# Mean squares of an RMS norm: squares taken by ScalarE from the PSUM bank, two halves of the features added by Pool, high and low parts in the rows of one product

## The chip, the cores and the metric

The kernel runs on one core of a Trainium2 chip. The metric is the device time of one execution in microseconds; the time before is the median of three runs. The engines are TensorE (PE for its products, PEld for its weight loads), VectorE (DVE), ScalarE (ACT), GpSimd (Pool or POOL) and the queue SP, which only issues DMAs. Each engine takes its instructions in the order in which the program lists them.

## The reference, cut to what matters

One layer of a streaming encoder with three groups of heads works on 1024 prompt tokens and 8 x 16 sample tokens. Group B is a differential attention with four heads, each 128 values wide. Its output goes through an RMS norm over the 128 features of a head, and that norm's mean of squares is what the change computes in another way:

```python
def diff_post(o, g, lambda_init):
    of = o.astype(jnp.float32)
    of = of * lax.rsqrt(jnp.mean(of * of, -1, keepdims=True) + RMS_EPS) * g.astype(jnp.float32) * (1.0 - lambda_init)
    return of.astype(o.dtype)
...
        o_b = diff_post(diff_attention_prompt(bq, bk, bv, lam), diff_subln_g[layer], lambda_init)
...
        s_b = diff_post(diff_core(tq, tk_all, tv_all, lam, None), diff_subln_g[layer], lambda_init)
```

The rest of the layer is one input projection (3584 columns), group A (banded attention, two units of two heads), group M (attention into 256 memory tokens, two units), a gate, an output projection and a layer norm.

## The kernel before, in words

Everything is float32. A product on TensorE takes float32r operands, and to keep float32 accuracy each operand is split into a high part (a float32r copy) and a low part (the value minus its copy). So each projection is three products into one bank (L155, L156, L157: high x high, low x high, high x low).

The work goes through eight units, in the order M0, B0, B1, B2, B3, A0, A1, M1. In each unit the attention over the prompt is the main stream, and projections (of gates, values, and the next unit's queries) are merged into it as fill; the 128 sample tokens of a unit are worked through in stages while the next unit's keys are projected. The program is written in that order, and a scheduler then reorders the instructions of each engine by its own estimate of times; so an edit of a few lines moves rows on every engine. What it makes of this change is shown below from the order of instructions.

For a B unit, `attention_b` goes over four pairs of 128 query columns. Scores are two products (L467, L468) into a bank of the pool `ps`; DVE takes the maximum (L604), ScalarE the exponential (L609). The weights are transposed by TensorE (L480) into a bank of the pool `pt` (two banks), split by ScalarE and DVE (L483/L487, L484/L488), and multiplied with the values into the one bank `po` (L643). When a pair is complete, `post_b` is called on the bank: it holds 128 features (partitions) by 256 tokens. `mean_square` queues the sum over the features as a product with a column of 1/128 (`mean`), so that the result is one row of 256 numbers; this small product is put between the products of a projection, or is forced out at the end of a pair. The row's bank is again `po`; DVE copies it to SBUF (L512) and SP stores it.

For the 128 sample tokens of a B unit, the last stage transposes the outputs (L908) into a `pt` bank, calls `post_b` on it with n = 128, and the row of mean squares goes into another `pt` bank. So the two banks of `pt` are shared by the sample's stages, by the transposes of the weights (L480) and by those of the values (L431): the next transposes wait until `post_b` has read the one bank and L512 the other.

In `post_b` before, ScalarE copies the bank to `od` (L495), Pool squares `od` (L499), ScalarE makes the float32r copy (L500), Pool the low part (L501), and TensorE takes two products, of the high and of the low part (L510). There are 4 pairs and 1 sample block in each of 4 units: 20 calls, 16 with n = 256 and 4 with n = 128.

At the end, the output projection (L1082) runs for nine tiles of 128 tokens; the first two are merged into the last unit. For a tile, `load` fetches its gates and mixed outputs back from DRAM, and `gated` scales them (L1049 on DVE).

Of the kernel before, what the change touches and what calls it, by code (L numbers as in the profile page):

```python
# [7 lines left out]
F32 = mybir.dt.float32  # L8
F32R = mybir.dt.float32r
AF = mybir.ActivationFunctionType  # L10
ALU = mybir.AluOpType
# [4 lines left out]
P = 128  # L16
# [59 lines left out]
def hybrid_step(tc, d, o):  # L76
    nc = tc.nc
    ctx = ExitStack()

    def pool(name, bufs=1, **kw):  # L80
        return Pool(ctx.enter_context(tc.tile_pool(name=name, bufs=bufs, **kw)))

    def f(ap):
        return ap.bitcast(F32)
# [22 lines left out]
    mean = const.tile([P, 1], F32R, tag="mean")  # L107
# [192 lines left out]
    tmp = pool("tmp", 2)  # L300
# [9 lines left out]
    for i in range(2):  # L310
        nc.vector.tensor_tensor(
            out=dl[:, i * 128 : i * 128 + 64], in0=dl[:, i * 128 : i * 128 + 64],
            in1=dl[:, i * 128 + 64 : i * 128 + 128], op=ALU.mult)
# [146 lines left out]
    def keep(u, a, b, od):  # L460
        nc.sync.dma_start(
            oscr[a // P : b // P, :, u.slot].rearrange("t p c -> p t c"), od.rearrange("p (t c) -> p t c", c=P))
# [29 lines left out]
    def post_b(u, po, c0, n):  # L492

        od = tmp.tile([P, n], F32, tag=f"od{n}", bufs=n // P)
        nc.scalar.copy(od, po)  # L495
        hi = tmp.tile([P, 256], F32R, tag="sqh", bufs=1)
        lo = tmp.tile([P, 256], F32R, tag="sql", bufs=1)
        sq = tmp.tile([P, 4, P], F32, tag="rs", bufs=2).rearrange("p a b -> p (a b)")[:, :n]
        nc.gpsimd.tensor_tensor(out=sq, in0=od, in1=od, op=ALU.mult)  # L499
        nc.scalar.copy(hi[:, :n], sq)  # L500
        nc.gpsimd.tensor_tensor(out=lo[:, :n], in0=sq, in1=f(hi)[:, :n], op=ALU.subtract)  # L501
        keep(u, c0, c0 + n, od)
        return hi, lo, sq[0:1]

    def mean_square(u, sq, ms, c0, n):


        def go():
            for x in range(2):
                nc.tensor.matmul(ms[:, :n], lhsT=mean, rhs=sq[x][:, :n], start=(x == 0), stop=(x == 1))  # L510
            row = sq[2]
            nc.vector.tensor_copy(row, ms[:, :n])  # L512
            nc.sync.dma_start(mscr[u.idx, c0 // P : (c0 + n) // P].rearrange("(o t) c -> o (t c)", o=1), row)

        tiny.append(go)
# [70 lines left out]
    def attention_b(u, need):  # L586
# [32 lines left out]
        def pair(j):  # L619
# [25 lines left out]
            def end():  # L645
                sq = post_b(u, st["po"], j * 256, 256)
                ms = ps_o.tile([1, 256], F32, tag="po")
                mean_square(u, sq, ms, j * 256, 256)
# [141 lines left out]
    def sample(u, kc_src, vc_src, nmask):  # L790
# [114 lines left out]
        def back():  # L905

            pt = ps_t.tile([P, P], F32, tag="pt")
            nc.tensor.transpose(pt, st["ot"], ident)  # L908
            if kind == "B":
                st["sq"] = post_b(u, pt, NPR, P)  # L910
            else:
                od = u.out[:, NPR:NTOK] if u.slot == 7 else tmp.tile([P, P], F32, tag="od128", bufs=1)
                nc.vector.tensor_copy(od, pt)
                if u.slot < 7:
                    keep(u, NPR, NTOK, od)
# [422 lines left out]
```

## Time and profile before

| | before |
|---|---|
| median of three runs | 669.27 us (666.96 to 670.08) |
| the profiled execution | 668.79 us, span 667.0 us from its first to its last instruction |
| PE busy | 653.6 us, 98% of the span |
| PEld busy | 611.0 us, 92% |
| DVE, ACT, POOL busy | 468.5 us (70%), 354.3 us (53%), 225.9 us (34%) |
| DMA | 78.91 MB, 118 GB/s on average |

Busy time is the time in which an engine had an instruction under way. The rows of products overlap each other, so PE's busy share doesn't say by itself that products follow each other at full rate; the distance from one product's start to the next one's does. The span is shorter than the execution's time by what lies around it, 1.8 us here.

### The profile page before, as it was taken

How to read it: one execution, taken by the hardware profiler on the slowest of the kernel's cores; microseconds unless marked ns; L12 is line 12 of the kernel's file. 1: busy time of each engine (PE TensorE's matmuls, PEld its weight loads, DVE VectorE, ACT ScalarE, POOL GpSimd, SP SyncE). 2: the span in 40 equal slices, each digit the busy share in tenths (PEclk: the TensorE clock that was granted, in tenths of full speed). 3: DMA queues.
4: the chain of work that ended last, by engine and by line, in shares of the span. 5: the costliest groups of instructions: out<-in, count | busy, mean ns of one | idle time of the engine just before them, and what ended most of it. 6: DMA issues, size and time to landing. Idle time of an engine off the chain costs nothing.

```text
span 667.0 us, 12222 instructions
## 1 busy us (share of the span) xinstructions
PE 653.6 (98%) x4306; PEld 611.0 (92%) x4306; DVE 468.5 (70%) x1173; ACT 354.3 (53%) x922; POOL 225.9 (34%) x278
## 2 busy tenths in 40 slices
PE   8999999999999999999999999999999999999995
PEld 7999999999899999998999999999999997887885
DVE  4769867787587757887477516674466688998755
ACT  5857854656455654566456635664466586211000
POOL 8253222642254223632324234332233142253101
PEclk9999999999999999999999999999999999999998
DMA  8951442121312232132312123132323747875311
GB/s 274 306 182 53 147 143 64 40 86 64 94 59 84 69 100 76 38 120 93 104 61 72 52 95 77 40 115 80 119 68 104 250 140 237 323 267 176 129 63 64
DMA packets 55837, 78.91 MB, mean 118 GB/s; under 512 B 9384, under 2 KB 33504, under 8 KB 55776
## 3 DMA queue, kind: packets, MB, share of 16 engines
q1 hardware_dynamic: 55488, 77.73, 35.3%
q8 instruction: 34, 0.56, 0.3%
q10 hardware_dynamic: 288, 0.39, 0.2%
q14 instruction: 27, 0.22, 0.1%
HBM read 57.69 MB, written 20.42 MB: 117 GB/s over the span
## 4 chain that ended last, share of the span: by engine, by line
PE 85%; DMA 6%; DVE 4%; issue 2%; ACT 1%; POOL 1%; SPq 0%; DVEq 0%; POOLq 0%; ACTq 0%
PE pp L155 15%; PE pp L157 15%; PE pp L156 15%; PE pp L1082 9%; PE ps L1082 6%; PE pt L480 5%; PE ps L467 4%; PE ps L468 4%; PE po L643 4%; PE po L682 3%; DMA rh<-in_wout 2%; PE pt L898 1%; DMA p<-mixed 1%; PE pt L431 1%; DMA mraw<-in_wmem 1%
## 5 line engine op out<-in xcount | busy, mean ns | idle before, releaser
L155 PE MATMUL pp<-xh,whi 128*128 128x384 f32 x594 | 203.7, 343 | 0.0
L156 PE MATMUL pp<-xl,whi 128*128 128x384 f32 x594 | 202.5, 341 | 0.0
L157 PE MATMUL pp<-xh,wlo 128*128 128x384 f32 x594 | 202.2, 340 | 0.0
L155 PEld LDWEIGHTS pp<-xh,whi 128*128 128x128 f32 x594 | 111.8, 188 | 2.7 <-DVE t L454 0.3
L156 PEld LDWEIGHTS pp<-xl,whi 128*128 128x128 f32 x594 | 111.8, 188 | 2.0 <-issue 0.2
L157 PEld LDWEIGHTS pp<-xh,wlo 128*128 128x128 f32 x594 | 111.8, 188 | 1.9 <-issue 0.3
L140 POOL TENSOR_TENSOR wlo<-wraw,whi 128x512 fp32r<-128x512 f32 x54 | 75.3, 1417 | 72.8 <-ACT whi L139 72.8
L609 ACT ACTIVATE p<-ps,nm 128x512 f32<-128x512 f32 (+3 forms) x96 | 55.2, 579 | 54.1 <-DVE nm L606 35.6
L467 PE MATMUL ps<-ka,qa 128*128 128x512 f32 (+4 forms) x176 | 58.6, 338 | 0.5 <-DVE nm L716 0.5
L468 PE MATMUL ps<-kl,qa 128*128 128x512 f32 (+4 forms) x176 | 57.4, 329 | 0.0
L480 PE MATMUL pt<-ident,p 128*128 128x128 f32 x332 | 54.9, 274 | 1.6 <-DVE ptl L484 0.8
L604 DVE TENSOR_REDUCE nm<-ps 128x1 f32<-128x512 f32 (+3 forms) x96 | 50.9, 549 | 4.0 <-PE ps L468 2.6
L724 POOL TENSOR_SCALAR p<-p,rs 128x640 f32<-128x640 f32 (+4 forms) x32 | 21.4, 671 | 68.7 <-DVE rs L723 52.7
L480 PEld LDWEIGHTS pt<-ident,p 128*128 128x128 f32 x332 | 39.9, 140 | 5.0 <-DVE ptl L484 2.1
L484 DVE TENSOR_TENSOR ptl<-pt,pth 128x512 fp32r<-128x512 f32 x56 | 38.3, 683 | 5.5 <-ACT pth L483 5.0
L483 ACT CAST pth<-pt 128x512 fp32r<-128x512 f32 x56 | 32.6, 586 | 17.3 <-PE pt L480 13.5
L1082 PE MATMUL pp<-xh,whi 128*128 128x512 f32 (+1 forms) x96 | 36.5, 380 | 0.0
L1082 PE MATMUL pp<-xl,whi 128*128 128x512 f32 (+1 forms) x96 | 36.2, 377 | 0.0
L1082 PE MATMUL pp<-xh,wlo 128*128 128x512 f32 (+1 forms) x96 | 35.8, 377 | 0.0
L139 ACT CAST whi<-wraw 128x512 fp32r<-128x512 f32 x54 | 30.9, 618 | 8.5 <-PE pp L156 4.5
L467 PEld LDWEIGHTS ps<-ka,qa 128*128 128x128 f32 x176 | 33.2, 189 | 1.8 <-DVE nm L716 0.7
L643 PE MATMUL po<-pth,va 128*128 128x256 f32 (+1 forms) x160 | 34.5, 284 | 0.0
(258 smaller groups left out, 1422.3 us busy)
## 6 DMA issues: line engine op xcount, KB each, us to landing
wraw<-in_win SPq DMA_DIRECT2D x54, 256.0 KB, 3.2
xr<-in_xT SPq DMA_DIRECT2D x12, 384.0 KB, 5.8
gates<-t SPq DMA_DIRECT2D x24, 192.0 KB, 2.2
qa<-in_xn SPq DMA_DIRECT2D x9, 512.0 KB
out_y<-qa SPq DMA_DIRECT2D x16, 256.0 KB, 2.2
mixed<-od SPq DMA_DIRECT2D x28, 128.0 KB, 2.3
p<-gates SPq DMA_DIRECT2D x7, 512.0 KB
p<-mixed SPq DMA_DIRECT2D x7, 448.0 KB
```

The source lines that it names most:

```text
L140: eng.tensor_tensor(out=lo[:, h], in0=raw, in1=f(hi[:, h]), op=ALU.subtract)
L155: nc.tensor.matmul(ps, lhsT=w[0][:, k], rhs=xh_[:, k], start=(k == 0), stop=False)
L156: nc.tensor.matmul(ps, lhsT=w[0][:, k], rhs=xl_[:, k], start=False, stop=False)
L157: nc.tensor.matmul(ps, lhsT=w[1][:, k], rhs=xh_[:, k], start=False, stop=(k == KT - 1))
L467: nc.tensor.matmul(ps, lhsT=u.qa[h][:, qs], rhs=u.ka[h][:, k0 : k0 + n], start=True, stop=False)
L468: nc.tensor.matmul(ps, lhsT=u.qa[h][:, qs], rhs=kl[h][:, k0 : k0 + n], start=False, stop=True)
L480: nc.tensor.transpose(pt[:, t, q * P : (q + 1) * P], p[q][:, cols[t][q] : cols[t][q] + P], ident)
L484: nc.vector.tensor_tensor(out=lo, in0=pt, in1=f(hi), op=ALU.subtract)
L604: nc.vector.tensor_reduce(out=nm[:, m, c : c + 1], in_=ps[c][:, : b - a], axis=AX.X, op=ALU.max, negate=True)
L609: nc.scalar.activation(e[:, a:b], ps[c][:, : b - a], AF.Exp, bias=nm[:, m, 0:1], accum_out=rs[:, m, c : c + 1])
L643: nc.tensor.matmul(out, lhsT=a, rhs=b, start=(g == 0 and x == 0), stop=(g == j and x == len(mm) - 1))
L1082: nc.tensor.matmul(y, lhsT=a[:, k], rhs=b[k][:, s], start=(k == 0 and x == 0), stop=(k == KT - 1 and x == 2))
```

## The change

The new `post_b` leaves `od` as it was. ScalarE squares the bank itself, in two instructions: features 0 to 63 into columns 0 to n-1 of the tile `sq`, and features 64 to 127 into columns 256 to 256+n-1, both on partitions 0 to 63. Pool adds the two halves (64 partitions by n). ScalarE puts the float32r copy of the sum into partitions 0 to 63 of one tile, `two`, and Pool writes the low part into partitions 64 to 127 of the same tile. One product with the column of 1/128 then sums the 64 high and the 64 low parts. The tile of low parts (`sql`) is gone.

```diff
         od = tmp.tile([P, n], F32, tag=f"od{n}", bufs=n // P)
         nc.scalar.copy(od, po)
-        hi = tmp.tile([P, 256], F32R, tag="sqh", bufs=1)
-        lo = tmp.tile([P, 256], F32R, tag="sql", bufs=1)
-        sq = tmp.tile([P, 4, P], F32, tag="rs", bufs=2).rearrange("p a b -> p (a b)")[:, :n]
-        nc.gpsimd.tensor_tensor(out=sq, in0=od, in1=od, op=ALU.mult)
-        nc.scalar.copy(hi[:, :n], sq)
-        nc.gpsimd.tensor_tensor(out=lo[:, :n], in0=sq, in1=f(hi)[:, :n], op=ALU.subtract)
+        sq = tmp.tile([P, 4, P], F32, tag="rs", bufs=2).rearrange("p a b -> p (a b)")
+        two = tmp.tile([P, 256], F32R, tag="sqh", bufs=1)
+
+        for h in range(2):
+            nc.scalar.activation(sq[0:64, 256 * h : 256 * h + n], po[64 * h : 64 * h + 64], AF.Square)
+        add = sq[0:64, 0:n]
+        nc.gpsimd.tensor_tensor(out=add, in0=add, in1=sq[0:64, 256 : 256 + n], op=ALU.add)
+        nc.scalar.copy(two[0:64, :n], add)
+        nc.gpsimd.tensor_tensor(out=two[64:128, :n], in0=add, in1=f(two)[0:64, :n], op=ALU.subtract)
         keep(u, c0, c0 + n, od)
-        return hi, lo, sq[0:1]
+        return two, sq[0:1, 0:n]
 
     def mean_square(u, sq, ms, c0, n):
 
 
         def go():
-            for x in range(2):
-                nc.tensor.matmul(ms[:, :n], lhsT=mean, rhs=sq[x][:, :n], start=(x == 0), stop=(x == 1))
-            row = sq[2]
+            nc.tensor.matmul(ms[:, :n], lhsT=mean, rhs=sq[0][:, :n], start=True, stop=True)
+            row = sq[1]
             nc.vector.tensor_copy(row, ms[:, :n])
```

The new file is two lines longer from here on, so that its L512 is the product (before L510), its L910 the sample's transpose (L908), its L611 the exponential (L609), its L1051 the scaling of a loaded tile (L1049); L431, L480, L467, L468, L484 and L495 keep their numbers or lie ahead.

The order of instructions shows where the product went. This is PE at the second sample block (that of unit B1, worked through during B2's projections; in the profile before at 248 us); `pt_3848` is the bank of the mean squares, `pt_3995` that of the value transposes. Before, the sample's transpose L908 stands 38 rows ahead of the first L510 here:

```order
L156 MATMUL pp_4335<-xl_28_124,whi_3574 128x384
L157 MATMUL pp_4335<-xh_27_123,wlo_3575 128x384
L510 MATMUL pt_3848<-sqh_3841,mean_88 1x128
L431 MATMUL pt_3995<-ident_81,t_621_3915 128x128 x2
L510 MATMUL pt_3848<-sql_3842,mean_88 1x128
L431 MATMUL pt_3995<-ident_81,t_621_3915 128x128
L155 MATMUL pp_4335<-xh_27_123,whi_3574 128x384
L156 MATMUL pp_4335<-xl_28_124,whi_3574 128x384
```

In the new file (the product's line is L512 there) the transpose stands 13 rows ahead of the product: eight projection products, of which the last is the first row here, and four products of scores.

```order
L157 MATMUL pp_4335<-xh_27_123,wlo_3575 128x384
L467 MATMUL ps_4251<-ka_578_3639,qa_548_3376 128x256
L468 MATMUL ps_4251<-kl_21_112,qa_548_3376 128x256
L467 MATMUL ps_4306<-ka_579_3640,qa_549_3377 128x512
L468 MATMUL ps_4306<-kl_22_113,qa_549_3377 128x512
L512 MATMUL pt_3849<-sqh_3842,mean_88 1x128
L431 MATMUL pt_3995<-ident_81,t_611_3915 128x128 x3
L480 MATMUL pt_4007<-ident_81,p_3932 128x128
L480 MATMUL pt_4007<-ident_81,p_3959 128x128 x2
```

One product is gone, the other has moved closer to the transpose, and the transposes of the weights (L480, into the bank that the row of mean squares must leave first) now follow at once. The same four score products, the product, three L431 and three L480 stand so at the third sample block of the new file (transpose 11 rows ahead of the product, 28 before) and at the first (12 rows; before 14, with the same rows around it). At the fourth the distance is 28 rows (37 before), four L480 and then three L431 follow the product, and these L431 take the bank.

ScalarE at the same place in the new file: `od_600` is the copy of the bank, `rs_3841` the squares, `sqh_3842` the tile of high and low parts.

```order
L611 ACTIVATE p_4202,rs_4130<-ps_4192,nm_4129 128x512
L611 ACTIVATE p_4202,rs_4130<-ps_4196,nm_4129 128x128
L495 COPY od_600_3839<-pt_3837 128x128
L500 ACTIVATE rs_3841<-pt_3837 64x128 x2
L503 CAST sqh_3842<-rs_3841 64x128
L453 ACTIVATE t_691_4331<-pp_4185 128x384
```

The two squares stand between the copy of the bank and the float32r copy; Pool's two instructions have the places that they had. The table load of ScalarE's functions stands in the order once, at the program's start, before and after.

The third place is DVE near the end of the last unit, where the tile t = 2 of the output projection is scaled; `p_9543` is what `load` fetched. Before:

```order
L1059 TENSOR_TENSOR wlo_9282<-kc_8888,whi_9281 128x128
L1059 TENSOR_TENSOR wlo_9296<-qa_1415_8895,whi_9295 128x128
L1049 SCALAR_TENSOR_TENSOR p_9543<-p_9543,subg_92,rs_9546 128x512
L484 TENSOR_TENSOR ptl_9335<-pt_9333,pth_9334 128x512
L667 TENSOR_TENSOR tab_1379_8705<-po_9155,po_1464_9230 64x256 x2
L484 TENSOR_TENSOR ptl_9350<-pt_9348,pth_9349 128x512
```

In the new file:

```order
L1061 TENSOR_TENSOR wlo_9282<-kc_8888,whi_9281 128x128
L484 TENSOR_TENSOR ptl_9335<-pt_9333,pth_9334 128x512
L1061 TENSOR_TENSOR wlo_9296<-qa_1395_8895,whi_9295 128x128
L1051 SCALAR_TENSOR_TENSOR p_9543<-p_9543,subg_92,rs_9546 128x512
L669 TENSOR_TENSOR tab_1359_8705<-po_9155,po_1444_9230 64x256 x2
L1091 SCALAR_TENSOR_TENSOR qa_1486_9433<-qa_1485_9431,pp_9319 128x512
```

One low part of transposed weights (L484 into `ptl_9335`), which PE needs, has moved ahead of the scaling, which waits for a DMA.

## Rows read from the trace of the kernel before

**Rows 1.** The page: busy time, share of the span, instructions of each engine.

```profile
PE 653.6 (98%) x4306; PEld 611.0 (92%) x4306; DVE 468.5 (70%) x1173; ACT 354.3 (53%) x922; POOL 225.9 (34%) x278
```

**Rows 2.** The page: share of the chain that ended last, by engine.

```profile
PE 85%; DMA 6%; DVE 4%; issue 2%; ACT 1%; POOL 1%; SPq 0%; DVEq 0%; POOLq 0%; ACTq 0%
```

**Rows 3.** Waits of PE: line, releaser, us in total, times, longest.

```profile
PE pt L480 <- DVE ptl L484: 0.8, 1, 0.8
...
PE pt L480 <- DVE rs L512: 0.6, 1, 0.6
```

**Rows 4.** Line L510 (source view): count, least, median, most ns; starts; form.

```profile
L510 PE MATMUL po<-sql,mean x16: 279/284/365, 111.5 to 388.0; 128*1 128x256 f32 x16
...
L510 PE MATMUL pt<-sql,mean x4: 303/304/309, 175.1 to 398.0; 128*1 128x128 f32 x4
```

**Rows 5.** Timeline of PE at 142.5 us: start, duration, line, operation.

```profile
142.51 0.28 PE L510 MATMUL po<-sqh,mean 128*1 128x256 f32 x1
142.63 0.34 PE L156 MATMUL pp<-xl,whi 128*128 128x384 f32 x1
142.81 0.34 PE L157 MATMUL pp<-xh,wlo 128*128 128x384 f32 x1
```

**Rows 6.** Timeline of PE at the first sample block, 172 to 177 us.

```profile
172.46 0.42 PE L155 MATMUL pp<-xh,whi 128*128 128x384 f32 x1
...
173.95 0.34 PE L157 MATMUL pp<-xh,wlo 128*128 128x384 f32 x1
...
174.83 0.22 PE L510 MATMUL pt<-sqh,mean 128*1 128x128 f32 x1
174.89 0.49 PE L431 MATMUL pt<-ident,t 128*128 128x128 f32 x3
175.14 0.30 PE L510 MATMUL pt<-sql,mean 128*1 128x128 f32 x1
176.09 0.55 PE L480 MATMUL pt<-ident,p 128*128 128x128 f32 x3 [0.65 <-DVE rs L512]
```

**Rows 7.** ACT's groups by form: busy, mean ns | idle before, releasers.

```profile
L609 ACT ACTIVATE p<-ps,nm 128x512 f32<-128x512 f32 x48 | 32.9, 688 | 41.1 <-DVE nm L606 35.6 <-DVE nm L604 5.3
...
L168 ACT ACTIVATE qa<-pp 64x256 fp32r<-64x256 f32 x6 | 2.3, 376 | 1.4 <-DVE qa L172 1.4
...
L385 ACT ACTIVATE sqz<-pp 64x128 f32<-64x128 f32 x6 | 1.6, 272 | 2.0 <-DVE qa L172 2.0
...
L218 ACT ACT_TABLE_LOAD x1 | 1.3, 1283 | 1.2 <-PEq L1317 1.2
```

**Rows 8.** Timeline of ACT at the first sample block.

```profile
172.74 0.27 ACT L495 COPY od<-pt 128x128 f32<-128x128 f32 x1 [1.03 <-PE pt L908]
...
175.42 0.49 ACT L453 ACTIVATE t<-pp 128x384 f32<-128x384 f32 x1 [1.55 <-PE pt L431]
175.81 0.47 ACT L437 CAST va<-pt 128x384 fp32r<-128x384 f32 x1
```

**Rows 9.** Timeline of POOL at the first sample block.

```profile
171.97 0.18 POOL L540 COPY r<-rs 128x1 f32<-128x1 f32 x1 [3.56 <-DVE rs L613]
...
173.95 0.46 POOL L501 TENSOR_TENSOR sql<-rs,sqh 128x128 fp32r<-128x128 f32 x1 [0.41 <-ACT sqh L500]
```

**Rows 10.** Timeline of DVE at the first sample block.

```profile
174.76 1.02 DVE L604 TENSOR_REDUCE nm<-ps 128x1 f32<-128x256 f32 x2
...
175.76 0.27 DVE L512 COPY rs<-pt 1x128 f32<-1x128 f32 x1
```

**Rows 11.** Timeline of PE at the fourth sample block.

```profile
398.00 0.30 PE L510 MATMUL pt<-sql,mean 128*1 128x128 f32 x1
398.14 0.39 PE L480 MATMUL pt<-ident,p 128*128 128x128 f32 x2
```

**Rows 12.** Timeline of DVE at the fourth sample block.

```profile
398.33 0.28 DVE L512 COPY rs<-pt 1x128 f32<-1x128 f32 x1 [9.61 <-PE pt L510]
```

**Rows 13.** Timeline of DVE near the end of the last unit.

```profile
561.97 0.75 DVE L1049 SCALAR_TENSOR_TENSOR p<-p,subg,rs 128x512 f32<-128x512 f32 x1 [0.72 <-DMA p<-mixed]
```

## The prediction

> **What bounds the kernel now.** I read the busy table first: PE is busy for 98% of the span, no other engine for more than 70% [rows 1]. A busy PE need not be an efficient one, so next the chain that ended last: 85% of it is PE's own work [rows 2]. Then the list of PE's waits: it has ten entries, the longest ones 0.8 us, once each, the two shown among them [rows 3]. So PE has almost nothing to wait for, and what counts is the distance from one product's start to the next. Two things can move the time: products taken off PE, and waits that a new order puts in front of it. One entry of that list matters here: PE waited for L512, the copy of the mean-square row, a single time in 20 calls [rows 3].
>
> **What is removed.** Twenty products: 16 low parts of 256 columns and 4 of 128 [rows 4]. The duration in these rows (284 and 304 ns) is not what they cost, since products overlap. At 142.51 us L510 starts, and the next product 0.12 us later, where a 384-column projection product takes 0.17 to 0.18 to the next start [rows 5]; the 128-column one takes 0.06, from 174.83 to 174.89 [rows 6]. So 16 x 0.118 + 4 x 0.06 = 2.1 us come off PE. That is the lower bound. At some places L510 stands among transposes and the distance is 0.20; I take that as debt of the transposes, which is paid wherever they are left. If it belongs to L510 at half of the places, 8 x 0.08 = 0.6 come on top: upper bound 2.8. I take 2.1.
>
> **What is added on ScalarE.** Two squares of 64 x n out of PSUM in each call. The trace has no Square, but it has ScalarE working on 64 rows from PSUM: 376 ns for 256 columns, 272 ns for 128 [rows 7]. Instructions of ScalarE overlap: one of 0.49 us is followed 0.39 later [rows 8]. So a square adds about 0.28 or 0.17, a call 0.55 or 0.35, and all 20 calls 16 x 0.55 + 4 x 0.35 = 10.2 us of ScalarE. It is cheap where ScalarE waits for others: before the 48 exponentials of 512 columns it was idle 41.1 us, 0.86 each, and nearly all of it for DVE's maximum [rows 7]. I cost this at nothing on PE for the 16 prompt calls. From below: no gain, since nothing is taken from ScalarE. From above: all of it, a rival below. Pool's two instructions keep their number and their free size; its add has two inputs as the subtraction had (0.46 us for 128 columns [rows 9]), and I cost the difference at nothing, with 0.1 us as bound. The float32r copy goes over 64 partitions instead of 128 with the same columns, and the same time.
>
> **What the longer chain delays.** The product needs both parts now, so it waits for the last Pool instruction, 0.35 (sample) or 0.55 us (prompt) later than the low part came before. For the 16 prompt calls PE never waited, and in the new order 31 to 74 rows stand between the pair's last value product and its mean square, as many or more than before (25 to 54), so I expect none. The four sample calls are the place to look, since there the order has moved the product closer to its transpose.
>
> Take the first one, which before had almost the new shape. The low part was ready at 173.95 + 0.46 = 174.41 [rows 9], PE came to L510 at 174.83 after nine projection products (172.46 to 173.95) and four of scores, needed L512's bank for L480 after the three L431, and started L480 at 176.09 [rows 6]. Without a wait L480 would have started at 174.83 + 0.06 + 3 x 0.11 + 0.06 = 175.28; so 0.8 us were lost here. What was late is L512: DVE took it at 175.76, behind two reductions that started at 174.76 when the scores were there [rows 10]. In the new order seven projection products stand ahead instead of nine. PE comes to the product at 174.83 - 2 x 0.174 = 174.48; the chain is ready at 174.41 + 0.35 + some 0.15 of handing over = 174.9; the reductions end 0.35 earlier too and L512 starts at 175.41, L480 at 175.75. The unhindered start would be 174.48 + 0.06 + 0.33 = 174.87: PE loses 0.87 us, about what it lost before. First block: nothing changes.
>
> At the second and third block PE did not wait before, since the list has one such wait in all [rows 3]. Now the order there is that of the first, so each loses the same: 2 x 0.87 = 1.7 us. At the fourth the product is far enough from its transpose, but the L431 behind four L480 need L512's bank; L512 started 0.33 us after the product and took 0.28 [rows 11, 12], so the bank is free 0.66 after the product's start, and the product with four L480 covers about 0.42: 0.24 us. Together 2.0 us are given back. Bounds: nothing, if the waits don't come; 3 x 1.3 + 0.3 = 4.2 if each chain is ready half a microsecond later than I think.
>
> **What the new order moves elsewhere.** About a third of PE's rows stand otherwise. I can point to one place: near the end of the last unit DVE waited 0.72 for a DMA to scale a tile [rows 13], a low part that PE needed stood behind that, and PE waited 0.8 for it [rows 3]. Now it stands ahead. The DMA is as late, and the next thing behind it is the sum that frees the bank `po`; so I credit half, 0.4 us, between nothing and 0.8. The rest I take as zero, with +-2 us for waits of the size of the ones in the list that come or go.
>
> **The sum.** Against the profiled execution, 668.79 us (span 667.0): -2.1 + 2.0 - 0.4 = -0.5, so 668.3. The median of the runs lies 0.48 above that execution, so 669.27 - 0.5 = 668.8 us. A difference under 0.5% (3.3 us) is about what a measurement of this kernel cannot tell from no change: the three runs alone span 3.1 us.
>
> **The rivals.**
>
> Products come off and nothing is given back. Speaks for it: PE is the bound and the chain is short. Against: the first sample block shows the wait in the very order that the others now have. Then -2.8 - 0.8: 665.7 us.
>
> ScalarE becomes the bound of the pairs (the other side). The two squares stand ahead of the exponentials in its queue, DVE's maxima and PE's transposes follow these, and PE runs out of fill. It decides once the 0.55 us exceed the idle time in front of an exponential; the mean idle is 0.86, so not at most of them, but the mean hides those with none. If nothing is hidden, +10.2 - 2.1: 677.4 us; if half, 672.3.
>
> Pool is late at the sample blocks. Its queue has the copy L540, which waits for DVE and through it for the exponentials, ahead of the sample's add. At the first block it ended at 172.15 [rows 9], and the new add could begin at 172.74 + 0.18 + 2 x 0.17, about 173.3 [rows 8]: a margin of 1.1 us. Each microsecond beyond it costs PE one at three places; with 1.2 us beyond, 668.8 + 3.6 = 672.4.
>
> The change switches ScalarE's tables. The row shows one table load, 1283 ns, for copies, exponentials and tanh together [rows 7]; if squares needed another one, 20 calls would cost two loads each, 40 x 1.28 = 51 us of ScalarE, and a time toward 700. The order of the new program still has the one load at its start, which nearly excludes this. The Trainium skill has such a rule in "ScalarE: Activation LUTs", section "Table sets: the hidden batching unit": functions are loaded as named sets, a function outside the loaded set needs a switch, and its table lists exp with tanh, relu and abs without naming square. It gives about 2.66 us for a switch ("What ACT_TABLE_LOAD costs"), by which the 40 switches would be 106 us. No run here shows a second load.
>
> **How the numbers follow.** The forecast, a balance of products and sample waits, has 0.62, with 666.5 to 671.2 as its own range. Nothing given back 0.17 (its time lies just beyond the bound of 0.5%; I count 0.11 of it as faster, 0.06 as same). ScalarE the bound 0.07, Pool late 0.06 (half of it beyond the bound), tables 0.01, and 0.07 for waits elsewhere that are larger than I allow, 0.03 faster and 0.04 slower. Faster 0.14, same 0.71, slower 0.15. The range from 665.3 to 672.9 leaves out about one in ten on each side.
>
> **What would show it.** L510's successor has 20 products, 0.12 us to the next start, and PE 4286 products. In the list of PE's waits the copy of the mean-square row should appear at the first three sample blocks (near 175, 247 and 324 us) with 0.4 to 0.9 us each, or the product itself should wait for Pool; Square should take about 0.38 and 0.27 us. The forecast is wrong if these waits are missing (then it is faster), if exponentials wait behind squares with PE idle after them, or if PE's lost time near 558 to 565 us grows.

## The result, and the profile after

The changed kernel takes 678.27 us (median of four runs, 677.05 to 679.07), the kernel before 669.67 on the same occasions: a ratio of 1.0131, with a 95% interval of 1.0114 to 1.0149. The change makes the kernel slower by 1.3%, 8.6 us. The forecast was 668.8, with a range to 672.9. The profiled execution's span grew from 667.0 to 675.7 us.

The busy table of the profile after, which answers to [rows 1]:

```profile
span 675.7 us, 12250 instructions
...
PE 657.3 (97%) x4286; PEld 612.0 (91%) x4286; DVE 476.3 (70%) x1173; ACT 364.9 (54%) x962; POOL 228.2 (34%) x278
```

The twenty products are gone, ScalarE is busy for 10.6 us more, and PE's share fell by one hundredth: it waits. The table hardly shows it, since a product's row lasts longer than its distance to the next one. The list of PE's waits, after (it answers to [rows 3]; per line the sum, the number and the longest):

```profile
PE pp L155 <- DVE t L454: 1.5, 4, 0.5
PE pt L261 <- POOL sqz L118: 1.1, 1, 1.1
PE ps L467 <- ACT p L774: 1.0, 1, 1.0
PE po L684 <- DVE tab L669: 1.0, 1, 1.0
PE po L684 <- ACT pth L487: 0.9, 1, 0.9
PE pt L512 <- POOL sqh L504: 0.7, 2, 0.5
PE pt L480 <- DVE rs L514: 0.7, 2, 0.4
PE po L684 <- ACT pth L483: 0.7, 1, 0.7
```

The wait of L261 stands in both lists with the same 1.1 us. Two groups are new. L512, L514 and L454 belong to the mean squares and to what stands around them. L774, L684, L669 belong to the last two units (A1 and M1) and the output projection, where no instruction of the change stands.

To see where the 8.7 us went I compared the traces at equal amounts of work: along PE's rows I summed the columns of all products but the mean-square ones, and took the difference of the start times where the sums are equal. It is worked out from all rows of PE, so only its sums stand here. In us against the kernel before:

| stretch of the kernel before | change |
|---|---|
| 0 to 71 us (input, first projections) | +0.3 |
| 71 to 474 us (units B0 to A0), of this: | +2.6 |
| - first, second, third, fourth sample block | +0.5, +1.5, +1.9, 0.0 |
| - the place at 223 to 236 us | +1.6 |
| - products that are gone | -2.1 (estimate: 16 x 0.1185 + 4 x 0.0585, the median distances to the next start) |
| - what is left: old waits that went | -0.8 |
| 474 to 594 us (units A1, M1, first output tiles), of this: | +5.8 |
| - 474 to 526, 526 to 550, 550 to 594 us | +0.8, +2.0, +3.0 |
| 594 us to the end | 0.0 |

**A sample block.** The second one, after, from the timeline (start, duration, in brackets the idle time and who ended it):

```profile
251.55 0.39 PE L468 MATMUL ps<-kl,qa 128*128 128x512 f32 x1
252.03 0.22 PE L512 MATMUL pt<-sqh,mean 128*1 128x128 f32 x1
252.09 0.52 PE L431 MATMUL pt<-ident,t 128*128 128x128 f32 x3
253.04 0.55 PE L480 MATMUL pt<-ident,p 128*128 128x128 f32 x3 [0.43 <-DVE rs L514]
253.78 0.44 PE L155 MATMUL pp<-xh,whi 128*128 128x384 f32 x1 [0.19 <-DVE t L454]
...
251.71 1.02 DVE L606 TENSOR_REDUCE nm<-ps 128x1 f32<-128x256 f32 x2
252.71 0.27 DVE L514 COPY rs<-pt 1x128 f32<-1x128 f32 x1
253.17 0.55 DVE L454 SCALAR_TENSOR_TENSOR t<-t,pp 128x384 f32<-128x384 f32 x1 [0.18 <-ACT t L453]
...
251.52 0.45 POOL L504 TENSOR_TENSOR sqh<-rs,sqh 64x128 fp32r<-64x128 f32 x1 [0.41 <-ACT sqh L503]
```

There are three waits in a row. The product waits 0.26 us for Pool's low part (from 251.77, when the scores are through, to 252.03). L480 waits for L514, which stands behind two reductions in DVE's queue: 0.62 more than three L431 take. Then the next projection waits 0.41 for its bank, which L454 frees, late behind L514. The low part is late by the length of the chain alone: Pool was idle for 0.41 us before it, until ScalarE's float32r copy was there. The prediction had the first two waits in one term and not the third.

**The place at 223 to 236 us:**

```profile
223.83 2.40 DVE L540 SCALAR_TENSOR_TENSOR p<-p,ri,p 128x1024 f32<-128x1024 f32 x1
...
223.72 0.18 POOL L542 COPY r<-rs 128x1 f32<-128x1 f32 x1
223.87 1.29 POOL L140 TENSOR_TENSOR wlo<-wraw,whi 128x512 fp32r<-128x512 f32 x1
225.09 1.18 POOL L542 COPY r<-srs 128x1 f32<-128x1 f32 x1
226.36 0.86 POOL L504 TENSOR_TENSOR sqh<-rs,sqh 64x256 fp32r<-64x256 f32 x1
...
227.27 0.28 PE L512 MATMUL po<-sqh,mean 128*1 128x256 f32 x1
229.14 0.38 PE L467 MATMUL ps<-ka,qa 128*128 128x256 f32 x1 [0.38 <-ACT p L611]
```

DVE and Pool hold each other up (the last section has the rows that show it), the low part is late by that, the product follows it, and DVE's delay reaches the exponentials, which free the bank that L467 needs.

**The last units.** SP, DVE and PE after, from the timeline:

```profile
524.93 0.38 SPq L455 DMA_DIRECT2D gates<-t  x1
530.65 0.42 SPq L455 DMA_DIRECT2D gates<-t  x1
531.17 0.46 SPq L1042 DMA_DIRECT2D kc<-gates  x1
...
537.01 1.09 DVE L1053 TENSOR_TENSOR kc<-tab,kc 128x896 f32<-128x896 f32 x1 [4.68 <-DMA kc<-gates]
571.21 0.75 DVE L1051 SCALAR_TENSOR_TENSOR p<-p,subg,rs 128x512 f32<-128x512 f32 x1 [0.88 <-DMA p<-mixed]
...
538.95 0.44 PE L155 MATMUL pp<-xh,whi 128*128 128x384 f32 x1 [0.41 <-DVE t L454]
542.45 0.63 PE L480 MATMUL pt<-ident,p 128*128 128x128 f32 x4 [0.30 <-DVE ptl L488]
546.06 0.33 PE L684 MATMUL po<-pth,va 128*128 128x128 f32 x1 [0.93 <-ACT pth L487]
564.15 0.39 PE L467 MATMUL ps<-ka,qa 128*128 128x256 f32 x1 [1.05 <-ACT p L774]
566.75 0.65 PE L480 MATMUL pt<-ident,p 128*128 128x128 f32 x4 [0.50 <-DVE ptl L484]
568.07 0.36 PE L684 MATMUL po<-pth,va 128*128 128x256 f32 x1 [0.67 <-ACT pth L483]
572.86 0.36 PE L684 MATMUL po<-pth,va 128*128 128x256 f32 x1 [1.00 <-DVE tab L669]
```

The load of the gates for output tile 0 is issued at 531.17, behind a store that was itself held up until 530.65 and that the load doesn't need (in the old order, below, the load stands ahead of it). DVE stands still for 4.68 us on the scaling that needs the load. Behind that stall PE waits three times, 1.6 us in all, up to 546.06. From 564 us on it waits four times in nine microseconds. The last of these is the place that the prediction credited with 0.4 us: L484 does stand ahead of the scaling L1051 now, but the scaling still waits 0.88 for its DMA, and PE waits 1.00 for the sum L669 behind it. Before, PE waited there 0.79 for L484 and 0.19 for the sum, so the wait only moved on.

ScalarE's groups after, by shape (busy time, mean ns, idle time before them):

```profile
L611 ACT ACTIVATE p<-ps,nm 128x512 f32<-128x512 f32 x48 | 33.0, 689 | 23.8 <-DVE nm L608 17.6 <-DVE nm L606 6.0
...
L500 ACT ACTIVATE rs<-po 64x256 f32<-64x256 f32 x32 | 12.2, 380 | 0.2
...
L500 ACT ACTIVATE rs<-pt 64x128 f32<-64x128 f32 x8 | 2.2, 272 | 0.0
...
L218 ACT ACT_TABLE_LOAD x1 | 1.3, 1283 | 1.2 <-PEq L1319 1.2
```

A square lasts as long as the neighbours in [rows 7] (380 and 272 ns against 376 and 272), and there is still one table load. But the two squares of a call start 0.39 or 0.28 us apart, not 0.28 or 0.17 as I took from overlapping instructions: by the distances of starts ScalarE's addition is 14.7 us, not 10.2 (the union of its overlapping rows, its busy time, grew by the 10.6 above). The idle time before the exponentials of 512 columns fell from 41.1 [rows 7] to 23.8 us.

### The profile page after: what moved, and what is told of

Read it like the earlier page. It is cut to its first block, busy times and chain, and to the rows that moved or that the text cites. A ratio compares the mean times of both kernels' runs of the same rounds, so it can differ in the third digit from the quotient of the medians.

```text
span 675.7 us, 12250 instructions
## 1 busy us (share of the span) xinstructions
PE 657.3 (97%) x4286; PEld 612.0 (91%) x4286; DVE 476.3 (70%) x1173; ACT 364.9 (54%) x962; POOL 228.2 (34%) x278
## 4 chain that ended last, share of the span: by engine, by line
PE 77%; DVE 10%; ACT 4%; DMA 4%; issue 3%; POOL 1%; SPq 0%; DVEq 0%; ACTq 0%; POOLq 0%
PE pp L155 13%; PE pp L156 13%; PE pp L157 13%; PE pp L1084 9%; PE ps L1084 6%; PE pt L480 4%; PE ps L467 3%; PE po L645 3%; PE ps L468 3%; PE po L684 3%; DMA rh<-in_wout 1%; PE pt L900 1%; DVE nm L606 1%; ACT p L611 1%; DVE t L369 1%
## 5 line engine op out<-in xcount | busy, mean ns | idle before, releaser
L155 PE MATMUL pp<-xh,whi 128*128 128x384 f32 x594 | 203.4, 342 | 1.7 <-DVE t L454 1.5
L155 PEld LDWEIGHTS pp<-xh,whi 128*128 128x128 f32 x594 | 111.8, 188 | 4.5 <-DVE t L454 2.9
L140 POOL TENSOR_TENSOR wlo<-wraw,whi 128x512 fp32r<-128x512 f32 x54 | 74.4, 1396 | 54.3 <-ACT whi L139 53.8
L611 ACT ACTIVATE p<-ps,nm 128x512 f32<-128x512 f32 (+3 forms) x96 | 55.4, 581 | 41.4 <-DVE nm L606 22.6
L467 PE MATMUL ps<-ka,qa 128*128 128x512 f32 (+4 forms) x176 | 58.7, 338 | 1.7 <-ACT p L774 1.0
L468 PE MATMUL ps<-kl,qa 128*128 128x512 f32 (+4 forms) x176 | 57.5, 329 | 0.0
L480 PE MATMUL pt<-ident,p 128*128 128x128 f32 x332 | 53.8, 274 | 1.8 <-DVE rs L514 0.7
L484 DVE TENSOR_TENSOR ptl<-pt,pth 128x512 fp32r<-128x512 f32 x56 | 38.3, 683 | 10.6 <-ACT pth L483 9.5
L480 PEld LDWEIGHTS pt<-ident,p 128*128 128x128 f32 x332 | 39.3, 140 | 5.5 <-DVE rs L514 1.5
L488 DVE TENSOR_TENSOR ptl<-pt,pth 128x256 fp32r<-128x256 f32 (+1 forms) x72 | 25.2, 352 | 22.1 <-ACT pth L487 21.5
L467 PEld LDWEIGHTS ps<-ka,qa 128*128 128x128 f32 x176 | 33.1, 188 | 4.0 <-ACT p L774 1.6
```

The lines of the kernel that those rows point to most:

```text
L140: eng.tensor_tensor(out=lo[:, h], in0=raw, in1=f(hi[:, h]), op=ALU.subtract)
L155: nc.tensor.matmul(ps, lhsT=w[0][:, k], rhs=xh_[:, k], start=(k == 0), stop=False)
L467: nc.tensor.matmul(ps, lhsT=u.qa[h][:, qs], rhs=u.ka[h][:, k0 : k0 + n], start=True, stop=False)
L468: nc.tensor.matmul(ps, lhsT=u.qa[h][:, qs], rhs=kl[h][:, k0 : k0 + n], start=False, stop=True)
L480: nc.tensor.transpose(pt[:, t, q * P : (q + 1) * P], p[q][:, cols[t][q] : cols[t][q] + P], ident)
L484: nc.vector.tensor_tensor(out=lo, in0=pt, in1=f(hi), op=ALU.subtract)
```

## The experiments

**Theory A:** the time is lost by the order of rows that the scheduler made, not by the change's own instructions. **Rival B:** ScalarE's squares and the longer chain cost it. They can be told apart because the order can be prescribed: for each pair of rows that should follow each other on an engine, the kernel adds a dependency that is an order only and no wait. The prescription itself costs nothing that shows: in the run of the two moved loads below, the rows of TensorE, VectorE, ScalarE and Pool come in the changed kernel's order one for one, and at equal work that run loses as much between 71 and 474 us, ahead of the moved loads, as the changed kernel does (within 0.1 us). The diff is the same for all kernels of this kind, only the table differs; their line numbers are 51 to 57 higher.

```diff
+ORDER = (
+    ...
+)
...
+    for e, steps in json.loads(zlib.decompress(base64.b64decode(ORDER))).items():
+        x, last = -1, None
+        for s in steps:
+            x += s
+            ins = rows[e][x]
+            if last is not None:
+                tc.add_manual_dep(ins, last.name, mybir.DependencyInfo(
+                    mybir.DependencyClass.NoSync, mybir.DependencyReason.DATA), reason="order")
+            last = ins
     ctx.close()
```

**Both codes in both orders.** The changed code in the old order:

> The changed kernel's instructions, each engine's in the order of the kernel before (the squares directly behind the copy of the bank, the product where the second of the two products stood, at the four sample calls where the first stood). Theory A, the time was lost by the new order of rows: 669.7 - 2.1 for the products + 0 to 2 for the sample blocks, 667.5 to 669.7 us. Rival B, the two squares and the longer chain themselves cost the time, whatever the order: 675 us or more.

The old code in the changed kernel's order:

> The kernel before, its instructions in the order of the changed kernel (both products where the one product stands, no squares). Theory A, order: 678.3 + 2.1 for the products that are there again, less some 1.5 for the shorter chain at the sample blocks, about 679 us. Rival B, squares and chain: 670 to 672 us.

| | old order | new order |
|---|---|---|
| old code | 1 (669.6 us) | 1.0088 (1.0071 to 1.0105), 675.7 us |
| changed code | 0.9978 (0.9963 to 0.9992), 667.8 us | 1.0131 (1.0114 to 1.0149), 678.3 us |

Theory A holds for the sign: in the old order the change is a small gain of 1.5 us, and the new order costs even the code that has no square at all 5.9 us. B holds for a part: in the new order the change costs another 0.43%, 2.9 us, though it saves 2.1 us of products. The old code in the new order came out 3.3 us below its expectation of about 679 us, which had put almost the whole loss on the order. Nor do the two effects add up: 5.9 for the order and -1.5 for the change make 4.4, and both together cost 8.6. The other 4.2 us arise only with both together, the longer chain in the new order. The old code in the new order shows the same waits in the last units as the changed kernel does (L519, L734, L719 there are L467, L684, L669 of the profile after; the first line is the row of mean squares at the sample blocks):

```profile
PE pt L532 <- DVE rs L564: 1.9, 3, 0.7
...
PE ps L519 <- ACT p L824: 1.0, 1, 1.0
PE po L734 <- ACT pth L539: 0.7, 1, 0.7
PE po L734 <- DVE tab L719: 0.7, 1, 0.7
PE po L734 <- ACT pth L535: 0.7, 1, 0.7
```

At equal work: in the last units +4.9 us with the old code in the new order, +0.9 with the changed code in the old one. At the first three sample blocks and the place at 223 us the new order costs the old code 0.2, 1.3, 1.5 and 0.6 us, the changed code 0.5, 1.5, 1.9 and 1.6. So of the blocks' losses most belongs to the order, and the longer chain adds 0.2 to 0.4 at a block and 1.0 at that place. In the old order it costs nothing at any of them. These differences make 1.9 us, and the last units 0.9; where the rest of what the change costs in the new order lies is not shown.

**Halves of the program.** Old order in the last units only, and old order ahead of them only:

> The changed kernel, in its own order up to the seventh unit; the rows of the last two units and of the output projection (1295 of PE's) take the order among themselves that they had before. No square and no mean-square product stands there. Theory A, order: the 6.0 us that the changed kernel lost from 460 us on come back, 672.3 us. Rival B: what is lost there comes from a late start of what stands ahead, 677 to 678 us.

> The complement: the changed kernel with the old order up to the attention of the seventh unit and its own order behind that. Theory A: the 2.7 us lost in the head come back and the products' 2.1 come off, less up to 1 for the sample blocks: 673.5 to 674.5 us, and the tail loses its 6 us as before. Rival B: 677 to 678 us, or the tail's loss goes with the head's.

674.16 us (1.007, 1.0056 to 1.0085) and 672.61 us (1.0047, 1.003 to 1.0065). The two losses add up and don't depend on each other: with the old head the last units lose 6.0 us, with the old tail 0.9. The old tail gave 1.9 less than expected since 1.7 us are lost at its seam, where the two orders meet. The old head came out 0.9 us below the range of its theory A: at the sample blocks, for which up to 1 us was left in it, nothing was lost.

**What the change itself costs, in the old order.** Each square computed twice, and the product computed twice:

```diff
-        for h in range(2):
+        for h in (0, 1, 0, 1):
             nc.scalar.activation(sq[0:64, 256 * h : 256 * h + n], po[64 * h : 64 * h + 64], AF.Square)
```

> The changed kernel in the order of the kernel before, with each square computed twice by ScalarE into the same place: 16 x 0.78 + 4 x 0.55 = 14.7 us more of ScalarE, and a chain that is 0.78 or 0.55 us longer. Theory A, ScalarE's work is hidden in this order but at the first sample block, where the chain is on the path: 668 to 669 us. Rival B, ScalarE's work in front of the exponentials is paid by half or more: 675 us.

```diff
-            nc.tensor.matmul(ms[:, :n], lhsT=mean, rhs=sq[0][:, :n], start=True, stop=True)
+            for _ in range(2):
+                nc.tensor.matmul(ms[:, :n], lhsT=mean, rhs=sq[0][:, :n], start=True, stop=True)
```

> The changed kernel in the order of the kernel before, with the product of high and low parts computed twice in succession: as many products as before the change. Theory A, a product costs its distance: 667.8 + 2.1 = 669.9 us. Rival B, a product between others is hidden: 667.8 us.

The products come to 669.86 us (1.0005, 0.9987 to 1.0023), by the medians 2.1 us above the 667.78 with one product, by the ratios 1.8: as expected. The second set of squares comes to 673.26 us (1.0053, 1.0037 to 1.0069), 5.5 us more by the medians and 5.0 by the ratios, neither the one nor the other: 14.7 us of ScalarE are hidden in this order, of the next 14.7 about a third is paid. This run lengthens the chain too, but of PE's waits between 71 and 480 us only one, of 0.5 us, is for Pool's low part; the others are for ScalarE and DVE. So the cover that I put in front of the squares is there, but it ends at about the amount that the change uses.

**Each half of the change alone,** in the order that the scheduler gives it. First ScalarE's square with the two products:

```diff
-        nc.gpsimd.tensor_tensor(out=sq, in0=od, in1=od, op=ALU.mult)
+        nc.scalar.activation(sq, po, AF.Square)
```

> One half of the change alone, in the order that the scheduler gives it: ScalarE squares the bank in one instruction of 128 rows in place of Pool's multiplication; the two products stay. The chain to the product is shorter than before. Its last two units come out in the changed kernel's order. Theory A, order: 5 us lost there and 1 to 3 at the sample blocks, 675 to 678 us. Rival B, what costs is the longer chain: 668 to 670 us.

Then the one product with Pool squaring:

```diff
         for h in range(2):
-            nc.scalar.activation(sq[0:64, 256 * h : 256 * h + n], po[64 * h : 64 * h + 64], AF.Square)
+            half = od[64 * h : 64 * h + 64]
+            nc.gpsimd.tensor_tensor(out=sq[0:64, 256 * h : 256 * h + n], in0=half, in1=half, op=ALU.mult)
```

> The other half: Pool squares the two halves of the features (two instructions of 64 rows) and adds them, one product takes high and low parts; ScalarE has no more to do than before. Its last two units come out in the changed kernel's order too. Theory A, order: 669.7 - 2.1 + 5 + 2 to 5, 675 to 678 us. Rival B, ScalarE's squares cost the time: 668 to 670 us.

673.29 us (1.0068, 1.0049 to 1.0087) and 681.51 us (1.0173, 1.0153 to 1.0193). The first lies between its two theories, the second above both. Both land in the same order of the last two units as the changed kernel (TensorE's last 1295 rows are the same one for one), and lose 5.6 and 6.7 us there. Ahead of that the kernel with the short chain loses nothing (-0.5 us between 71 and 474). The one with three Pool instructions ahead of the float32r copy loses 7.0, of which 6.6 around the second sample block, where PE waits 2.2 us for an exponential too, so not all of it is the product's wait. ScalarE has the least to do in the slowest of these kernels: its squares as such are not what costs the time.

**Is any new order bad?** One constant of the merge of main stream and fill altered, in the kernel before and in the changed one:

```diff
-LEAD = 4.25
+LEAD = 4.4
```

> The kernel before with nothing changed but one constant of the merge of main stream and fill (LEAD 4.4 for 4.25), which gives another order of rows from the second unit on. Theory A, the order of the kernel before is a good one among many and most others cost microseconds: 671 to 677 us. Rival B, orders differ little and the changed kernel's is a bad exception: 668.5 to 670.5 us.

> The changed kernel with the same constant of the merge altered (LEAD 4.4 for 4.25), which gives it another order in the last two units, unlike that before and unlike its own. Theory A, the loss in the last units belongs to the one order that the changed kernel got there: that part (5 to 6 us) comes back and the sample blocks and the place at 226 us still cost their 4 to 5, 671 to 674 us. Rival B, the change leads to that loss in whatever order: 677 us or more.

The kernel before gets a little faster, 668.2 us (0.9983, 0.9968 to 0.9997): theory A's claim that most other orders cost microseconds gets no support from this one. The changed kernel comes to 672.14 us (1.0045, 1.0026 to 1.0063), inside A's range, but partly by luck: its last units lose 2.7 us instead of 5.8, so 3 us come back there and not 5 to 6, and the other 3 come back ahead of them, where A expected none (at equal work -0.6 us between 71 and 474 instead of +2.6; the sample blocks and the place at 226 us cost some 2 and not 4 to 5). All three edits of this place got the bad order of the last units, and one constant takes the changed kernel out of half of its loss: the order doesn't belong to the change.

**What in the last units' order costs it.** The two loads of gates moved ahead in SP's order:

> The changed kernel in its own order, but for two rows of SP's: the loads of the gates of output tiles 0 and 1 stand directly behind the last store that they need, as they did before, instead of behind five further DMAs. Theory A, VectorE's queue stood still for 4.7 us behind the scaling that needs these loads, and TensorE ran out of work behind it: up to 2.3 us come back, 676 us. Rival B, TensorE's own order of rows in the last unit is what waits: 678 us, no change.

675.65 us (1.0088, 1.0062 to 1.0115). By the medians 2.6 us come back, at equal work in the last units 1.1 (5.8 to 4.6): the late loads are a part, and not the larger one. DVE now waits 1.62 us for the gates (L1105 is L1053):

```profile
534.05 1.09 DVE L1105 TENSOR_TENSOR kc<-tab,kc 128x896 f32<-128x896 f32 x1 [1.62 <-DMA kc<-gates]
```

By stretches, 526 to 550 us falls from 2.0 us to 0.4, and 550 to 594 us stays at 3.0 to 3.2. The kernel with the other constant above has it the other way round: 2.4 us in the first and 0.6 in the second. So the last units lose at two places, and only the first of them follows the loads. In the old order (changed code) this load was issued at 522.68, ahead of those stores, and DVE waited 2.48 (L1098 and L1109 there):

```profile
522.68 0.32 SPq L1098 DMA_DIRECT2D kc<-gates  x1
...
526.22 1.09 DVE L1109 TENSOR_TENSOR kc<-tab,kc 128x896 f32<-128x896 f32 x1 [2.48 <-DMA kc<-gates]
```

With more rows moved:

> The changed kernel in its own order, but for: the two loads of gates ahead, as before; six products of the output projection that stood in one block ahead of the last unit's transposes stand three each behind two later groups of transposes, where TensorE waited with nothing to do; and at two prompt calls Pool's low part stands ahead of a small copy that waits for VectorE. Theory A, the new order had put its fill ahead of the waits: loads 2.3 to 2.9, fill 1.0, Pool 0.4 come back from 678.3, 674 to 674.6 us. Rival B, the last unit's chain of VectorE and ScalarE sets the time there and the six products' place doesn't matter: as with the loads alone, 675.7 us.

675.87 us (1.0095, 1.008 to 1.011): no better than the loads alone, as B said. The output products now stand where PE had waited, and PE waits elsewhere (4.1 us are still lost). Pool's row, moved ahead, took the product's wait away, and the wait of the scores behind it grew to 0.56 (L519 is L467):

```profile
225.98 0.28 PE L564 MATMUL po<-sqh,mean 128*1 128x256 f32 x1
...
228.06 0.39 PE L519 MATMUL ps<-ka,qa 128*128 128x256 f32 x1 [0.56 <-ACT p L663]
```

SP's and Pool's order alone set back in the last units:

> As the kernel with the old order in its head (672.6 us, of which 5.5 are lost in the last two units), but in the last two units SP and Pool keep the old order too; only TensorE, VectorE and ScalarE have the changed kernel's order there. Theory A, what stands still there is VectorE and ScalarE behind loads that SP issues late: most of the 5.5 us come back, 667.5 to 669 us. Rival B, it is the order of the computing engines' own rows: 671.5 to 672.6 us.

682.49 us (1.0196, 1.0166 to 1.0226). Both theories fall here. The old order of loads was made for the old order of their readers; with the new one ScalarE waits 11.1 us for a half row of the output weights, and PE behind it:

```profile
PE po L741 <- ACT pth L544: 7.4, 2, 5.8
```

```profile
ACT xh L1208 <- DMA rh<-in_wout: 11.1, 2, 6.7
```

So this run doesn't tell which engine's order costs the 5.8 us; it shows that in these units the queue's order and the readers' order only work as a pair.

**A version that beats both.** The changed code in the old order, with three rows moved:

> The changed kernel in the order of the kernel before, with three rows moved: at the first sample block the copy of the mean-square row stands between the two reductions of VectorE; VectorE's scaling of the loaded tile 2 stands four rows later; ScalarE's copy of a loaded half row of the output weights stands behind the split that TensorE waits for. Theory A: 667.8 less 0.5, 1.2 and 0.6 = 665.5 us. Rival B: each wait only moves on to the next row, 667 to 668 us.

667.03 us (0.9964, 0.9947 to 0.9981), against 0.9978 without the three moves; the intervals overlap. At equal work the two moves in the last units bring 0.8 us, and that at the sample block nothing, because the wait moved on. PE there, without the move and with it (L536 is L480 and L211 is L155, the lines that wait in the block above; L570 and L510 there are L514 and L454):

```profile
175.15 0.55 PE L536 MATMUL pt<-ident,p 128*128 128x128 f32 x3 [0.61 <-DVE rs L570]
```

```profile
174.96 0.55 PE L536 MATMUL pt<-ident,p 128*128 128x128 f32 x3
176.10 0.45 PE L211 MATMUL pp<-xh,whi 128*128 128x384 f32 x1 [0.60 <-DVE t L510]
```

## Why the prediction was wrong

**The list of PE's waits** was misread: its longest entry before is L261 for Pool, 1.1 us once, not 0.8. It is the same after, so nothing of the sum hangs on it.

**The products** were right: 1.8 to 2.1 us by the run with the product twice; in the kernel after, the median distance from such a product to the next start is 0.1185 and 0.0585 us.

**The squares on ScalarE** were rightly costed at nothing on PE as far as the old order goes, with a wrong size beneath (14.7 us for 10.2), and with less in reserve than the mean idle time let me believe.

**The prompt calls,** costed at no wait, were right for fourteen of sixteen. At 227 and 304 us the product waited for Pool. The distance in rows that I counted says how much cover stands there, not whether Pool comes in time; Pool stood behind a small copy that waited for DVE.

**The sample blocks,** 2.0 us, cost 3.9. The mechanism was right: the new order puts the product close to its transpose and the L480 behind it, and L514 stands behind the reductions. The size was not, because the chain of waits was followed for two steps only. The third, L155 for the bank that L454 frees, begins right behind L480 at 176.09, with which I ended the first block [rows 6]. Block by block, 0, 0.87, 0.87 and 0.24 were forecast, and 0.5, 1.5, 1.9 and 0.0 measured. The order alone, with the old code, costs 0.2, 1.3 and 1.5 of the first three.

**The step that failed** is the term for what the new order moves elsewhere: a credit of 0.4 us at one place, "the rest I take as zero, with +-2 us". A third of PE's rows had moved; I worked out one place near 562 us, where the move looked good, and took the rest as balanced. The last units lost 5.8 us, and at the credited place the wait only moved on, from 0.79 and 0.19 to 1.00. The two orders of the last units differ by 4.9 us whichever code runs, more than any term that I worked out. In the chances it had 0.04 on the slower side. The cause is settled as far as the order of rows in the last units: changed code in the old order loses 0.9 us there, old code in the new order 4.9. Of the rows, the late loads of gates carry a part (1.1 us). How the rest divides among the engines stays open: the one run that exchanged the order of single engines made a mismatch that cost more than what it looked for.

Of the rivals, "ScalarE becomes the bound" gave nearly the time (677.4) by a mechanism that the runs exclude as the main one: in the old order the same squares cost nothing. That Pool's queue is held up came true at two prompt calls; at the sample blocks Pool was idle before the low part, and what made the product wait there (0.26 us at the second) was the longer chain. The table switch did not occur: the one load serves copies, exponentials, tanh and squares.

## What to carry to other kernels

Where a scheduler orders the rows, an edit is two changes, and they can be priced apart: run the new code in the old order and the old code in the new one. When predicting, a reordering that spans a third of the rows needs a variance from other orders of the same program, not a zero; here a single constant moved the changed kernel by 5.8 us and the kernel before by 1.1 (by the ratios). And among the first rows to look up in a new order are loads that come to stand behind stores: DVE, which takes its rows in order, stood still for 4.68 us at the first reader of such a load.

## What the runs showed of the hardware that was not expected

DVE's instruction of 128x1024 with two inputs in SBUF takes 1.28 us at 369.62 us of the changed kernel, with no Pool instruction beside it, and 2.40 at 223.83 above. There Pool's L140 runs from 223.87 to 225.16, no longer than it does elsewhere (mean 1.40 us over 54), and DVE's instruction ends 1.07 after that. Pool's next instruction, a copy of one column that takes 0.18 us elsewhere, then takes 1.18 and ends with DVE's. The two engines took turns, each for a whole instruction. The Trainium skill states such a rule in "SBUF — State Buffer", section "Who interferes with whom": a VectorE instruction with two inputs in SBUF shares its second read interface with GpSimd, and one of the two waits for the other's instruction to end. The trace agrees that one waits for the whole of the other. The section adds that the order of issue decides which one waits. DVE's row at 223.83 starts 0.04 us ahead of L140's and is the late one, but Pool's copy ahead of L140 (223.72 to 223.90) was still under way then. Where no Pool row was, as in the kernel before at 144.63, DVE's took its usual time and Pool's waited:

```profile
144.63 1.26 DVE L538 SCALAR_TENSOR_TENSOR p<-p,ri,p 128x1024 f32<-128x1024 f32 x1
...
144.69 2.35 POOL L140 TENSOR_TENSOR wlo<-wraw,whi 128x512 fp32r<-128x512 f32 x1 [2.28 <-ACT whi L139]
```

For this change it means that moving work between ScalarE, DVE and Pool also moves who waits for whom there, which no count of busy time shows.
